# The residual's reordered copies to memory: from GpSimd beside the scans to ScalarE, in part one stage earlier

## The chip, the cores and the metric

The kernel runs on one core of a Trainium2 chip. A core has five instruction streams that run side by side and wait for each other by semaphores: TensorE (PE, with its weight loads as PEld), VectorE (DVE), ScalarE (ACT), GpSimd (POOL) and SyncE (SP), and sixteen DMA engines that serve the transfers issued by SP, ACT and POOL. The metric is the device time of one execution in microseconds.

## The reference, cut to what matters

The program is one step of a two-layer diffusion backbone on 1024 latent tokens and 128 context tokens of width 1024. Layer 0 mixes tokens by a short convolution and a Fourier transform; layer 1 mixes them by a bidirectional state-space scan (S5). Each layer has a gated feed-forward part behind its mixer, and each part adds to the residual `x`:

```python
h = modulate(rmsnorm(x, p['norm1_g'][l]), sh1, sc1)
m, fin = s5_mixer(h, ...)                # layer 1: scans forward and backward
x = x + g1 * m
h = modulate(rmsnorm(x, p['norm2_g'][l]), sh2, sc2)
x = x + g2 * swiglu(h, p['w_ffn_in'][l], p['w_ffn_out'][l])
```

So the residual that leaves layer 0's feed-forward part is read twice: normalised, as the input of the scans, and unchanged, when the scans' gated output is added to it.

## The kernel before, in words

The residual lies in SBUF as `xall`, eight feature tiles (`x[0]` to `x[7]`) of 128 partitions by 1152 tokens. Three chunks of 384 tokens (`CW`, chunk numbers 0 to 2; the last has 256 latent and 128 context tokens) are the unit of work of layer 0.

**End of the feed-forward stage of layer 0.** `last_outer` goes chunk by chunk: for each of eight output tiles TensorE makes six products, VectorE adds them to `xall` (L599, `update`), ScalarE squares the result (L192, tile `sq`, or `ssq` for the first of a chunk), and GpSimd sums the squares (L196). Three `sq` buffers are in use. When a chunk's eight squares are there, TensorE sums them over partitions (L205, `nst`), VectorE makes the reciprocal root in small steps (L207, L163 to L169), TensorE spreads it (L217, `nrb`), VectorE multiplies (L1022, tile `t`, four buffers), and ScalarE scales, shifts and reorders the tokens into `u` (L1025: one instruction of 384 tokens a tile, for the last chunk two of 256 and 128). This last part is `S5In.chunk(ch)`, called through `per_chunk` for chunks 0 and 1, and directly for chunk 2.

**Entry of the scans.** Each complete `u` tile goes to memory (`u_d<-u`, issued by SP) and comes back with another partition layout (`U<-u_d`). The tiles of `u` lie in slots that the scans use later as `D`, `re` and `tp`, so the scans' first writes wait until the stores have read them. `front(f)` makes input products (tile `S`) that ScalarE copies into `D` (L1143, with small start values by L1145 and L1146).

**Scans.** For each of eight feature tiles f, VectorE runs `scan(f)`: six elementwise products and sums (L1151 to L1156), two `TENSOR_TENSOR_SCAN` instructions (L1169), six more of the first kind. The first and last tile go in halves of 584 elements, the others have 1168. `back(f)` makes outputs `Y`, `gelu(f)` writes them over `xall[f]`; so the residual must have left `xall[f]` before. That is what `spill(f)` does: GpSimd copies tile f of the residual in the order of the scans' tokens to a tile `xs` (L1211, 1024 and 128 tokens) and sends it to memory `x_d` (L1213), from where `Glu.load_x` takes it after the scans (L1272). `run` issues `spill(f)` in turn f of its loop, with `issue_after` holding it behind the last sum of squares.

The order on each engine is made by the tile framework, not by the order of the calls alone: it places instructions by when it expects them to be able to run, and adds the waits. ScalarE, VectorE and GpSimd then run their streams strictly in that order.

Of the kernel before, what the change touches and what calls it, by code (L numbers as in the profile page):

```python
# [11 lines left out]
F32 = mybir.dt.float32  # L12
# [7 lines left out]
D = 1024  # L20
# [21 lines left out]
def segments(lo, hi):  # L42
    """the parts of a range of tokens by conditioning."""
    out = []
    if lo < LAT:
        out.append((lo, min(hi, LAT), 0))
    if hi > LAT:
        out.append((max(lo, LAT), hi, 1))
    return out
# [7 lines left out]
def kernel(  # L57
# [30 lines left out]
    # ---------------------------------------------------------------- constants  # L88
# [19 lines left out]
    # ---------------------------------------------------------------- helpers  # L108
# [24 lines left out]
    class Pools:  # L133
# [9 lines left out]
        def s(self, p, dt=F32):  # L143
            """short-lived tiles, apart from the long-lived ones where they have slots of their own."""
            return self.act.tile([128, CW], dt, tag="s", name=nm(p), bufs=self.ns) if self.ns else self.a(p, dt)
# [11 lines left out]
    # rsqrt(v) by Newton from an integer seed  # L157
# [17 lines left out]
    def unpermuted(fn, dst, src, ch):  # L175
        """context tokens back from (t, c) order."""
# [6 lines left out]
    class Norm:  # L183
        """means of squares of a chunk's tokens, three blocks of tokens with one per partition."""
# [28 lines left out]
    def spread(r):  # L213
        """rstd of three blocks of tokens from a column per block to every partition."""
# [5 lines left out]
    def modulated_tile(P, x, rb, f, ch, l, which):  # L220
        """x * rstd * scale + shift of a tile, in its two parts; rb covers the chunk."""
# [10 lines left out]
    def modulated(P, norm, ch, xs, l, which, h):  # L232
        """in parts, a tile each."""
# [8 lines left out]
    # ---------------------------------------------------------------- conditioning  # L242
# [22 lines left out]
    def ada_slice(P, s):  # L265
        """a slice of layer 0's conditioning map, off the tensor engine but for the sum over partitions;
        in two parts, to be issued some time apart. The rows go through memory to one feature per partition."""
# [18 lines left out]
    def ada_columns(l, b0, nb, src, t):  # L286
        """blocks of 128 outputs, from memory to one per partition."""
# [9 lines left out]
    def ada_block(pool, l, s, raw, nrow=2):  # L297
        """in two parts, to be issued some time apart."""
# [11 lines left out]
    def ada_rows(pool, s, raw):  # L310
        """a block of layer 1's conditioning map, the rows of the four groups of products to memory."""
# [8 lines left out]
    def ada_sums(pool, b0, nb):  # L320
        """sums of the four groups, one output per partition."""
# [21 lines left out]
    # ---------------------------------------------------------------- entry  # L343
    def start(P, st, x, h):
        """x to one feature per partition, its norm, modulation and the first two tiles of the
        input projection, a feature tile at a time as the conditioning arrives."""
# [96 lines left out]
    # ---------------------------------------------------------------- layer 0 mixer  # L443
    def mixer(P, big, x, h, norm2, hn, first):
# [10 lines left out]
        def four_in(i):  # L455
# [5 lines left out]
            # folded about 512 and 256: sums of even and odd outputs for cosine, then sine, and the middle  # L461
# [140 lines left out]
    # ---------------------------------------------------------------- feed forward  # L602
    def ffn(P, l, x, h, norm_next, steps=None, nsteps=0, at_end=None, per_chunk=None):
# [32 lines left out]
        def last_outer(j0):  # L636
            """the last two, a chunk of tokens at a time."""
# [25 lines left out]
    # ---------------------------------------------------------------- S5 tables  # L663
# [10 lines left out]
    def exp_poly(pool, x, n):  # L674
        """exp of an fp32 array by range reduction and a polynomial."""
# [21 lines left out]
    def sincos(pool, a, n):  # L697
        """sine and cosine of an fp32 array, reduced by parts of 2 pi that multiply exactly."""
# [36 lines left out]
    def state_layout(dst0, dst1, dup):  # L735
        """[(d, p), g] from dup[(d, g), p twice]."""
# [269 lines left out]
    # ---------------------------------------------------------------- S5 layer  # L1006
    class S5In:
        """modulated input of the S5 layer, a chunk of tokens at a time."""
# [24 lines left out]
    class S5:  # L1033
# [40 lines left out]
        def parts(f):  # L1074
            """the first and the last tile go through in halves."""
# [762 lines left out]
```

## Time and profile before

| what | value |
|---|---|
| time, median of 3 runs | 2558.5 us |
| lowest and highest run | 2555.06 and 2559.73 us |
| profiled execution, first to last instruction (span) | 2550.3 us |
| median less that span | 8.2 us |
| TensorE clock, mean granted | 0.978 of full speed |
| busy: PE, DVE, ACT, POOL | 95%, 70%, 36%, 10% |

The profile is of one execution. The time of that execution itself is not listed apart from the three runs; the 8.2 us between its span and the median lie before the first and after the last instruction, and the sums below are made on the span with these 8.2 us added. A share of busy time is a mean over stages that have different limits, so the stages that the change touches are read by windows and by instructions in order of time.

### The profile page before, as it was taken

How to read it: one execution, taken by the hardware profiler on the slowest of the kernel's cores; microseconds unless marked ns; L12 is line 12 of the kernel's file. 1: busy time of each engine (PE TensorE's matmuls, PEld its weight loads, DVE VectorE, ACT ScalarE, POOL GpSimd, SP SyncE). 2: the span in 40 equal slices, each digit the busy share in tenths (PEclk: the TensorE clock that was granted, in tenths of full speed). 3: DMA queues.
4: the chain of work that ended last, by engine and by line, in shares of the span. 5: the costliest groups of instructions: out<-in, count | busy, mean ns of one | idle time of the engine just before them, and what ended most of it. 6: DMA issues, size and time to landing. Idle time of an engine off the chain costs nothing. (4 is left out here: it accounts for less than half of the span.)

```text
span 2550.3 us, 44262 instructions
## 1 busy us (share of the span) xinstructions
PE 2426.1 (95%) x16815; PEld 2360.4 (93%) x16815; DVE 1789.7 (70%) x4641; ACT 906.2 (36%) x1915; POOL 252.0 (10%) x256
## 2 busy tenths in 40 slices
PE   7999999999999999999956789999999999989998
PEld 6999999999999999999946679998999999989998
DVE  7765678787787778887869984558766666644444
ACT  5322443233222322223364443435232232434333
POOL 0000120000000000000124421112000000122110
PEclk9999999999999999999978889999999999999999
DMA  9443342244444444443457954433222222466543
GB/s 258 127 137 96 92 116 61 68 122 122 123 115 123 122 114 130 115 131 115 116 195 221 261 177 147 120 103 103 74 77 69 88 62 86 147 204 189 162 132 124
DMA packets 503093, 327.96 MB, mean 129 GB/s; under 512 B 99144, under 2 KB 472448, under 8 KB 502880
## 3 DMA queue, kind: packets, MB, share of 16 engines
q1 hardware_dynamic: 330208, 233.10, 30.8%
q10 hardware_dynamic: 163680, 58.96, 9.6%
q0 software_dynamic: 8992, 33.07, 3.9%
q8 instruction: 133, 2.18, 0.4%
q14 instruction: 80, 0.66, 0.1%
HBM read 254.04 MB, written 71.01 MB: 127 GB/s over the span
## 5 line engine op out<-in xcount | busy, mean ns | idle before, releaser
L123 PE MATMUL mm<-hh,whi 128*128 128x384 f32 x1392 | 472.6, 339 | 1.1 <-ACT f L459 1.1
L125 PE MATMUL mm<-hh,wlo 128*128 128x384 f32 x1392 | 466.4, 335 | 0.0
L124 PE MATMUL mm<-hl,whi 128*128 128x384 f32 x1392 | 465.3, 334 | 0.0
L117 DVE TENSOR_TENSOR wlo<-wraw,whi 128x1024 fp32r<-128x1024 f32 (+1 forms) x216 | 259.8, 1203 | 243.5 <-ACT whi L116 240.2
L116 ACT ACTIVATE whi<-wraw 128x1024 fp32r<-128x1024 f32 (+1 forms) x218 | 226.0, 1037 | 506.3 <-PE mm L124 383.5
L123 PEld LDWEIGHTS mm<-hh,whi 128*128 128x128 f32 x1392 | 261.3, 188 | 11.2 <-issue 9.2
L125 PEld LDWEIGHTS mm<-hh,wlo 128*128 128x128 f32 x1392 | 261.3, 188 | 2.9 <-issue 2.5
L124 PEld LDWEIGHTS mm<-hl,whi 128*128 128x128 f32 x1392 | 261.5, 188 | 0.0
L599 DVE SCALAR_TENSOR_TENSOR xall<-mm,modt,xall 128x384 f32<-128x384 f32 (+2 forms) x416 | 203.6, 510 | 60.3 <-PE mm L125 59.4
L123 PE MATMUL mm<-hb,whi 128*128 128x384 f32 x528 | 179.9, 341 | 11.3 <-ACT whi L116 11.2
L1534 PE MATMUL mm<-T,wf 128*128 128x288 f32 x640 | 189.4, 296 | 0.0
L1535 PE MATMUL mm<-T,wf 128*128 128x288 f32 x640 | 188.8, 295 | 0.0
L1536 PE MATMUL mm<-T,wf 128*128 128x288 f32 x640 | 188.2, 294 | 0.0
L125 PE MATMUL mm<-hb,wlo 128*128 128x384 f32 x528 | 179.4, 340 | 2.0 <-DVE wlo L117 1.9
L123 PE MATMUL mm<-hidh,whi 128*128 128x384 f32 x528 | 180.0, 341 | 0.0
L124 PE MATMUL mm<-hb,whi 128*128 128x384 f32 x528 | 178.6, 338 | 0.0
L125 PE MATMUL mm<-hidh,wlo 128*128 128x384 f32 x528 | 176.6, 334 | 0.0
L124 PE MATMUL mm<-hidl,whi 128*128 128x384 f32 x528 | 176.5, 334 | 0.0
L196 POOL TENSOR_TENSOR ssq<-ssq,sq 128x384 f32<-128x384 f32 (+1 forms) x78 | 100.1, 1284 | 686.9 <-ACT sq L192 683.7
L123 PE MATMUL mm<-zz,whi 128*128 128x288 f32 x512 | 151.5, 296 | 2.4 <-ACT zz L1267 2.4
L124 PE MATMUL mm<-zz,whi 128*128 128x288 f32 x512 | 150.8, 295 | 0.3
L125 PE MATMUL mm<-zz,wlo 128*128 128x288 f32 x512 | 150.4, 294 | 0.3 <-DVE wlo L117 0.3
(391 smaller groups left out, 5710.5 us busy)
## 6 DMA issues: line engine op xcount, KB each, us to landing
wraw<-in_w_ffn_out_dram SPq DMA_DIRECT2D x70, 512.0 KB
wraw<-in_w_ffn_in_dram SPq DMA_DIRECT2D x52, 512.0 KB
araw<-in_w_ada_dram ACTq DMA_DIRECT2D x48, 512.0 KB
wraw<-in_w_glu_dram SPq DMA_DIRECT2D x32, 512.0 KB
araw<-in_w_ada_dram ACTq DMA_DIRECT2D x80, 192.0 KB
wraw<-in_w_out_mix_dram SPq DMA_DIRECT2D x24, 512.0 KB
xall<-in_w_ffn_in_dram SPq DMA_DIRECT2D x20, 512.0 KB
wr<-in_w_ffn_in_dram SPq DMA_DIRECT2D x20, 512.0 KB
```

Of the source, the lines that this page charges most:

```text
L116: S.activation(hi[:, :n], raw[:, :n], AF.Copy)
L117: eng.tensor_sub(lo[:, :n], raw[:, :n], hi[:, :n].bitcast(F32))
L123: PE.matmul(ps, wh, xs[0], start=start, stop=False)
L124: PE.matmul(ps, wh, xs[1], start=False, stop=False)
L125: PE.matmul(ps, wl, xs[0], start=False, stop=stop)
L196: self.last = G.tensor_add(self.ssq[ch], self.ssq[ch], sq)
L599: V.scalar_tensor_tensor(x[o][:, a:b], ps[:, a - ch * CW:b - ch * CW], gate(l, which, o, s), x[o][:, a:b], op0=OP.mult, op1=OP.add)
L1534: PE.matmul(ps, wh, xh[:, cs], start=kt == 0, stop=False)
L1535: PE.matmul(ps, wh, xl[:, cs], start=False, stop=False)
L1536: PE.matmul(ps, wl, xh[:, cs], start=False, stop=kt == NFK - 1)
```

## The change

`spill` is made per tile and chunk, on ScalarE. Its copy writes a tile `xs` of 384 tokens from a pool of three buffers of its own; the store is still issued by GpSimd, now as a strided one: for latent tokens, each of eight rows of a tile's image in `x_d` gets 48 tokens (192 bytes) of chunk 0 or 1, or 32 tokens (128 bytes) of chunk 2; the context tokens are one run of 512 bytes. Chunks 0 and 1 are copied in `per_chunk`, in the feed-forward stage right after the chunk's `S5In.chunk`; chunk 2 is copied in the scans' loop. The `yz` pool of the scans has four slots where it had five. The core of the diff (comments taken out of other places are left away):

```diff
-        BUFS = {"U": 3, "T": 4, "d0": 2, "D": 4, "re": 3, "tp": 1, "yz": 5}
+        BUFS = {"U": 3, "T": 4, "d0": 2, "D": 4, "re": 3, "tp": 1, "yz": 4}
...
-        def spill(self, f):
-            xs = self.t("yz", "xs")
-            for a, b in ((0, LAT), (LAT, TOK)):
-                G.tensor_scalar(xs[:, a:b].rearrange("p (t c) -> p t c", t=T8),
-                                self.x[f][:, a:b].rearrange("p (c t) -> p t c", t=T8), 1.0, 0.0, op0=OP.mult, op1=OP.add)
-            nc.gpsimd.dma_start(x_d[f], xs[:, :TOK])
+        def spill(self, f, ch):
+
+            lo, hi = ch * CW, (ch + 1) * CW
+            xs = self.pools[0].tile([128, CW], F32, tag="xs", name=nm("xs"), bufs=3)
+            for a, b, ctx_ in segs(ch):
+                n = (b - a) // T8
+                part = xs[:, a - lo:b - lo].rearrange("p (t c) -> p t c", t=T8)
+                S.activation(part, self.x[f][:, a:b].rearrange("p (c t) -> p t c", t=T8), AF.Copy)
+                base, c0, wd = (LAT, 0, NC_CTX) if ctx_ else (0, a // T8, NC_LAT)
+                dst = x_d[f][:, base:base + T8 * wd].rearrange("p (t c) -> p t c", t=T8)[:, :, c0:c0 + n]
+                nc.gpsimd.dma_start(dst, part)
...
-                with tc.issue_after(self.after):
-                    self.spill(f)
+                self.spill(f, NCH - 1)
...
             def per_chunk(ch):
                 s5["in"].chunk(ch)
+                for f in range(NF):
+                    s5["run"].spill(f, ch)
```

Where the copies come to stand is the framework's doing. On ScalarE, around the end of chunk 1's scaling, the stream of before reads as follows (`u` is the scaled tile, `sq` the square of a residual tile of chunk 2, `d` a decay table that is needed later; the words in brackets are the engines or DMA queues waited for):

```order
L1125 ACTIVATE d_15741<-smask,rho 128x146
L192 ACTIVATE sq_15571<-xall 128x384 [waits DVE_49,Pool_49]
L1125 ACTIVATE d_15741<-smask,rho 128x146
L192 ACTIVATE sq_15611<-xall 128x384 [waits DVE_49,Pool_49]
L1025 ACTIVATE u_15217<-t_15578,modt_87,scalet_89 128x8x48 [waits DVE_49]
...
L1025 ACTIVATE u_15224<-t_15599,modt_87,scalet_89 128x8x48 [waits DVE_49]
L1025 ACTIVATE u_15217<-t_15658,modt_87,scalet_89 128x8x32 [waits DVE_49]
L1025 ACTIVATE u_15217<-t_15658,modt_87,scalet_89 128x8x16
```

And in the changed kernel, at the same place (`L1215` is the new copy; `DMASW` are the stores that GpSimd issues):

```order
L1025 ACTIVATE u_15217<-t_15602,modt_87,scalet_89 128x8x48 [waits DVE_49]
L192 ACTIVATE sq_15595<-xall 128x384 [waits Activation_49,Pool_49]
...
L1025 ACTIVATE u_15224<-t_15623,modt_87,scalet_89 128x8x48 [waits DVE_49]
L1215 ACTIVATE xs_15635<-xall 128x384 [waits DMASW0_49,Activation_49]
L1215 ACTIVATE xs_15638<-xall 128x384 [waits DMASW1_49,Activation_49]
L1215 ACTIVATE xs_15641<-xall 128x384 [waits DMASW2_49,Activation_49]
L192 ACTIVATE sq_15659<-xall 128x384 [waits Pool_49]
L1125 ACTIVATE d_15789<-smask,rho 128x146 x4
L1215 ACTIVATE xs_15644<-xall 128x384 [waits DMASW3_49,Activation_49]
L1215 ACTIVATE xs_15647<-xall 128x384 [waits DMASW4_49,Activation_49]
L1025 ACTIVATE u_15217<-t_15706,modt_87,scalet_89 128x8x32 [waits DVE_49]
```

The last two squares of chunk 2 stood ahead of the eight `u` of chunk 1; now one stands behind the first of them and the last behind all eight and three copies. Ahead of this place the stream has eleven more copies: five between the squares of chunk 1, three behind the eight `u` of chunk 0, three between the squares of chunk 2.

The second place is ScalarE's stream at the entry of the scans. Before, the copies of `S` to `D` for tile 0 followed the start values directly:

```order
L1145 ACTIVATE D_15750<-h_15213 128x2 x3
L1143 ACTIVATE D_15750<-S_15752 128x2x145 [waits PE_49]
...
L1143 ACTIVATE D_15751<-S_15760 128x2x145 [waits PE_49]
L1146 ACTIVATE D_15751<-h_15214 64x2 [waits Activation_49]
L1143 ACTIVATE D_15750<-S_15768 128x2x145 [waits PE_49]
```

Now three pairs of copies of chunk 2 stand ahead of them, and three more pairs between the eight `D<-S` of tile 0, each pair behind the two stores of the pair three before it:

```order
L1145 ACTIVATE D_15798<-h_15213 128x2 x3
L1215 ACTIVATE xs_15972<-xall 128x256 [waits DMASW5_49]
...
L1215 ACTIVATE xs_16293<-xall 128x128
L1143 ACTIVATE D_15798<-S_15800 128x2x145 [waits PE_49]
...
L1143 ACTIVATE D_15799<-S_15808 128x2x145 [waits PE_49]
L1215 ACTIVATE xs_16454<-xall 128x256 [waits DMASW1_49,DMASW0_49]
...
L1143 ACTIVATE D_15798<-S_15848 128x2x145 [waits PE_49]
L1215 ACTIVATE xs_16776<-xall 128x256 [waits DMASW5_49,DMASW4_49]
L1146 ACTIVATE D_15798<-h_15213 64x2 [waits Activation_49]
L1143 ACTIVATE D_15799<-S_15856 128x2x145 [waits PE_49]
```

The last `D<-S` of tile 0, the row at the end, thus stands behind the copy that waits for the third pair's stores. VectorE's and TensorE's streams keep their order, but for a few neighbouring products. On GpSimd the 16 copies and 8 stores of before are replaced by 32 stores (16 of chunks 0 and 1, 16 of chunk 2), all ahead of the first `zp<-yd_d`.

## Rows read from the trace of the kernel before

**Rows 1.** The page, busy time of the engines over the whole span.

```profile
PE 2426.1 (95%) x16815; PEld 2360.4 (93%) x16815; DVE 1789.7 (70%) x4641; ACT 906.2 (36%) x1915; POOL 252.0 (10%) x256
```

**Rows 2.** Windows: length, then busy PE, PEld, DVE, ACT, POOL; PEclk, DMA share, GB/s.

```profile
1270.50:1281.60 11.10, 9.81 (x63) 9.49 (x62) 8.55 (x23) 7.67 (x23) 7.29 (x8) 1.00 0.39 158
1281.60:1297.40 15.80, 9.06 (x55) 8.39 (x53) 13.07 (x35) 13.16 (x22) 6.70 (x7) 0.87 0.50 167
1297.40:1307.60 10.20, 3.13 (x14) 2.68 (x14) 7.56 (x22) 7.89 (x8) 6.25 (x7) 0.50 0.36 109
1317.70:1328.60 10.90, 8.84 (x120) 8.49 (x116) 2.80 (x4) 8.68 (x43) 0.00 (x0) 0.86 1.03 407
1328.60:1506.20 177.60, 127.47 (x992) 121.35 (x992) 177.53 (x137) 66.48 (x234) 70.33 (x27) 0.85 0.78 227
```

**Rows 3.** Timeline of DVE in the scans: start, duration, instruction (us).

```profile
1356.14 1.35 DVE L1156 TENSOR_TENSOR D<-D,D 128x1168 f32<-128x1168 f32 x1
...
1376.53 3.15 DVE L1156 TENSOR_TENSOR D<-D,D 128x1168 f32<-128x1168 f32 x1
...
1466.23 3.15 DVE L1156 TENSOR_TENSOR D<-D,D 128x1168 f32<-128x1168 f32 x1
...
1487.01 2.54 DVE L1155 TENSOR_TENSOR re<-T,re 128x584 f32<-128x584 f32 x1
1489.48 0.98 DVE L1152 TENSOR_TENSOR tp<-T,D 128x584 f32<-128x584 f32 x1
...
1499.70 0.73 DVE L1155 TENSOR_TENSOR re<-T,re 128x584 f32<-128x584 f32 x1
...
1503.64 2.53 DVE L1156 TENSOR_TENSOR D<-D,re 128x584 f32<-128x584 f32 x1
```

**Rows 4.** Timeline of POOL: the copy of residual tile 1.

```profile
1365.62 14.34 POOL L1211 TENSOR_SCALAR xs<-xall 128x1024 f32<-128x1024 f32 x2
```

**Rows 5.** Groups by shape on ACT, 1260 to 1560 us (L939: all): count, busy us, mean ns.

```profile
L1025 ACT ACTIVATE u<-t,modt,scalet 128x384 f32<-128x384 f32 x16 | 16.1, 1087 | 2.4 <-DVE t L1022 2.4
L192 ACT ACTIVATE sq<-xall 128x384 f32<-128x384 f32 x21 | 10.6, 518 | 5.8 <-POOL ssq L196 2.9 <-DVE rq L167 1.8 <-DVE xall L599 0.6
L939 ACT ACTIVATE io<-fx 128x256 f32<-128x256 f32 x64 | 42.0, 708 | 67.3 <-DMA e_d<-io 55.9 <-DMA acol<-ada_d 3.6 <-DVE tt L833 3.5
```

**Rows 6.** Timeline of ACT at the end of the feed-forward stage.

```profile
1274.87 1.02 ACT L1125 ACTIVATE d<-smask,rho 128x146 f32<-128x146 f32 x3
...
1281.63 8.19 ACT L1025 ACTIVATE u<-t,modt,scalet 128x384 f32<-128x384 f32 x8
...
1297.47 7.89 ACT L1025 ACTIVATE u<-t,modt,scalet 128x384 f32<-128x384 f32 x8 [2.39 <-DVE t L1022]
1307.67 10.08 ACT L1025 ACTIVATE u<-t,modt,scalet 128x256 f32<-128x256 f32 x16 [2.31 <-DVE t L1022]
```

**Rows 7.** Timeline of PE and DVE: the sum of squares and the reciprocal root.

```profile
1273.01 0.28 PE L205 MATMUL nst<-ones,ssq 128*128 128x1 f32 x2
...
1274.44 0.16 DVE L207 TENSOR_SCALAR v<-nst 128x3 f32<-128x3 f32 x1 [0.61 <-PE nst L205]
...
1302.00 0.15 DVE L207 TENSOR_SCALAR v<-nst 128x3 f32<-128x3 f32 x1
1302.19 1.00 DVE L163 TENSOR_SCALAR rq<-v 128x3 int32<-128x3 int32 x1
...
1307.08 2.54 DVE L1022 TENSOR_TENSOR t<-xall,nrb 128x384 f32<-128x384 f32 x5 [1.13 <-PE nrb L217]
```

**Rows 8.** Stores and loads issued by POOL (L1272, L1630): ns min/median/max, and landing of L1630.

```profile
L1272 POOL DMA_DIRECT2D xall<-x_d x4: 884/892/917, 1524.8 to 1537.8; - x4
...
L1630 POOL DMA_DIRECT2D hr<-hid_d x46: 537/539/557, 2218.1 to 2431.6; - x46
...
DMA to landing us min/median/max: 2.6/4.3/8.1
```

**Rows 9.** Timeline of DVE at the entry of the scans.

```profile
1328.60 1.44 DVE L1152 TENSOR_TENSOR tp<-T,D 128x584 f32<-128x584 f32 x2 [1.46 <-DMA u_d<-u]
```

## The prediction

> **What bounds the kernel now.** I read the page first: TensorE is busy for 95% of the span, VectorE for 70%, GpSimd for 10% [rows 1]. That is a mean over stages, so I next cut the span into windows around the change [rows 2]. The reader should see three stages. From 1270 to 1297 us TensorE still ends the feed-forward part while ScalarE squares, scales and reorders. From 1297 to 1328.6 us nothing is kept busy: this is a chain of short steps from the last square of chunk 2 to the first scan, and ScalarE's stream is a part of it. From 1328.6 to 1506.2 us VectorE is busy for 177.53 of 177.60 us: the scans are bound by VectorE alone. Behind it, TensorE's next products need the scans' last outputs. So a microsecond added to the chain, or taken from VectorE's scans, is one of the whole; what happens on GpSimd counts only through these two.
>
> **What the change removes: GpSimd's copies beside the scans.** VectorE's own timeline shows their price [rows 3]. The same instruction (`D<-D,D`, 1168 elements) took 1.35 us at 1356.14, where GpSimd had no copy, and 3.15 us at 1376.53 and in each tile up to 1466.23, five times in all. In that time GpSimd's copy is recorded as busy for 14.34 us [rows 4], nearly all of it waiting; it gets through once a tile and then holds VectorE up. The period of a tile without a copy is 1376.53 - 1356.14 = 20.39 us; with one it is (1466.23 - 1376.53) / 4 = 22.43. Five tiles give 5 x 2.04 = 10.2 us. In tile 6 two instructions take 2.54 and 0.98 us, where their kind takes about 0.74 each (0.73 in the row at 1499.70): 2.0 us. In tile 7 one takes 2.53 in place of 0.74: 1.8 us. Together **14.0 us** leave the scans. Nothing else should take the place of VectorE there: ScalarE is busy for 66.48, TensorE for 127.47 of the 177.60 us, the DMA engines for 0.78 of them [rows 2], and the tile from 1356.14 on ran its 20.39 us without a gap.
>
> **What it adds: sixteen copies ahead of the last scaling.** The trace has no such copy, so I bound its price [rows 5]. An instruction of 384 tokens in plain order takes 0.52 us (`sq`), one that reorders as the copy does, but also scales and shifts, 1.09 us (`u`); a plain copy that permutes 256 elements takes 0.71. In a row, instructions start about 0.1 us earlier than the last one ends (eight `u` in 8.19 us, three `d` in 1.02) [rows 6]. The copy has `u`'s strides without its two operands, so I take 0.95 us, a pitch of **0.85 us**, between bounds of 0.43 and 1.01.
>
> Each copy needs one of three buffers, so it also waits for the store of the copy three before it. GpSimd needs 0.89 us to issue a transfer of 1024 pieces [rows 8]. The landing of a transfer of the same size (192 KB) lies between 2.6 and 8.1 us, median 4.3; the pieces of that one are longer, though. I take **4 us after the issue**.
>
> Now the chain on ScalarE, in three stretches.
>
> *To the first `u` of chunk 0 (1281.63).* Five copies, 4.3 us. ScalarE is idle there for 11.10 - 8.55 = 2.6 us [rows 2], and eight small fills of about 2 us in all move further back. The fourth copy waits for the first store and comes about half a microsecond late: **+0.5 us**.
>
> *To the first `u` of chunk 1 (1297.47).* Six copies, 5.1 us, 0.9 us of the fills moved here, 0.9 us for the ninth copy, which waits for the sixth's store, and the 0.5 from before. Against that stands the idle time of 15.80 - 13.16 = 2.6 us: **+4.8 us**.
>
> *To the first `u` of chunk 2 (1307.67).* Before, this took 10.2 us: the eight `u` of chunk 1 and a gap, since the last square of chunk 2 was made earlier and its root waited only for VectorE. In the new order the last square stands behind those eight `u` and three copies, and the chain begins there. So: eight `u` at 1.01, two squares at 0.42, three copies at 0.85 make 11.5 us; then the sum on TensorE 1.4 (1273.01 to 1274.44), the root 2.4, the spread 1.1, the product and its hand-over 0.6 (1307.08 to 1307.67) [rows 6, 7]. The root took 3.95 us before (1307.08 - 1.13 - 1302.00); its first two steps took about 1.0 us each beside GpSimd's fills, 0.8 more than the 0.2 of such a step (1302.00 to 1302.19). The fills now come later, so I count 2.4, with 3.95 as the bound. Sum 17.0 less 10.2: **+6.8 us**. The last two copies, with four fills, take 2.9 us under this chain as long as their stores land in time.
>
> So the last scaling starts 0.5 + 4.3 + 6.8 = **11.6 us** later (the 4.8 contains the 0.5). With it go the stores of `u`, on which the first scan waits [rows 9].
>
> **What it adds at the entry of the scans.** The last `D<-S` of tile 0 stands behind the copy that waits for the third pair of chunk 2's stores. Counted from the end of the last `u`: 1.0 us to the first pair's first half, three pairs of stores at 0.9 + 0.6 us on GpSimd, 4 us of landing, 1.1 us of work, 10.6 us. VectorE needs that tile at its second `tp` product, 0.7 us after 1328.60, 11.5 us after the last `u` ended. At 4 us of landing this costs nothing; but the DMA engines are full just then (share 1.03, [rows 2]), so landings nearer 6 us, and `u`'s own stores delayed by these packets, are likely: 0 to 3 us, I take **+2 us**. The last pairs of copies of chunk 2 and the smaller `yz` pool have VectorE's 20 us per tile to hide in; without that cover the pairs would cost their 2 us. The stores of chunks 0 and 1 need no time of the path beyond the waits counted.
>
> **Sum.** 2550.3 - 14.0 + 11.6 + 2.0 = 2549.9 us of span; with 8.2 us around it, **2558 us**, against a median of 2558.5. The gain in the scans is paid back ahead of them. About 0.2%, or 5 us, is what a measurement of this kernel can tell from no change.
>
> **The rivals.**
>
> *Slow landings (slower).* With three buffers, a copy that waits for its store holds up what stands behind it three times on the path: the fourth copy before a square of chunk 1, the ninth before squares of chunk 2, the fifteenth before the last scaling. Beyond about 4.5 us after the issue, each further microsecond costs three. At 6 us the chain is 16.5 late and the entry 3: 2558.5 + 5.5 = 2564; at 8 us, the upper end of the row, 22.5 and 3: 2570. It decides from 6 us on. For it: stores of 1024 pieces of 192 bytes, when no row of the trace shows one with pieces so short. Against it: at 1281 to 1307 us the DMA engines are half idle (0.50 and 0.36) [rows 2]. The Trainium skill gives a rule for each side in "DMA: Bandwidth & Descriptors": by its fit (section "Anatomy of one DMA — SWDGE (gpsimd) path") such a store would need about 2.0 us plus 0.45, an estimate by which no copy waits and the chain would be 10.7 us late; by its section "Specifications" pieces under 512 bytes are read, modified and written, which would make it longer. The row of 2.6 to 8.1 us [rows 8] bears out neither for such pieces.
>
> *Cheap copies (faster).* If the reordering read costs nothing, a copy has a pitch of 0.43 us. Then the second stretch is +2 us, the third 8.1 + 0.8 + 1.3 + 5.5 - 10.2 = +5.5, and the chain some 7.5 to 8.5 us late. With nothing lost at the entry this is 2558.5 - 14.0 + 8 = 2552.5. The `u` row, twice the plain price, speaks against it.
>
> *The scans don't get shorter.* If loads of the tables or the outputs were the true limit at 22.4 us a tile, the 14 us would not come back, and the time would be 2558.5 + 13.6 = 2572. The tile of 20.39 us and VectorE's lack of any gap speak against it.
>
> **Chances.** No change by the sum above 0.54, slow landings 0.24, cheap copies 0.16, scans not shorter 0.06. In the first case the time lies between 2553.5 and 2563. Slower than by 0.2%: 0.24 + 0.06, less a little for the mild end of slow landings, 0.28; faster 0.17; within it 0.55. The range of 2552.5 to 2567 leaves out the dear end of the slow landings and the last case.
>
> **What would show it.** Right: `D<-D,D` with a mean of 1.36 us in the scans, a tile period of 20.4 us, L1215 at 0.85 to 1.0 us, the first `u` of 256 tokens at about 1319, the second `tp` product at about 1343, the last scan work ending near 1506 as before. Wrong: waits of ScalarE on stores ahead of L1215 of more than a few microseconds in sum; VectorE idle between scans; or the last square of chunk 2 well before 1312.

## The result, and the profile after it

The changed kernel took 2569.5 us in the median of 12 runs (2559.76 to 2578.11); the kernel before, beside it on the same chip, 2556.6 us (12 runs, 2550.61 to 2560.71). The ratio is 1.0054, with a 95% interval of 1.0041 to 1.0066: 14 us slower. The forecast was no change, 2558.0 us; the time lies above the upper end of its range.

The profiled execution of the changed kernel has a span of 2558.9 us and took 2561.05 us, so some 2.2 us lie around a span, not the 8.2 us that the forecast added. By an estimate from that, the profile of before is one of an execution of some 2552.5 us, near the lowest of its runs; sums are better made on differences.

To place the 14 us, the program around the change is cut at seven events that both traces have. Each event is the start of an instruction, but for the last scan work, which is taken at the end of the last `D<-D,re`. The first `tp` product starts at 1328.60 before and at 1349.43 in the changed kernel; the expectation of e11 calls it the second.

| stretch | before | changed | difference | forecast |
|---|---|---|---|---|
| first square of chunk 0 to first `u` of chunk 0 | 17.31 | 19.49 | +2.2 | +0.5 |
| to first `u` of chunk 1 | 15.84 | 20.59 | +4.75 | +4.3 |
| to first `u` of chunk 2 | 10.20 | 17.44 | +7.2 | +6.8 |
| to the first `tp` product | 20.93 | 27.42 | +6.5 | +2 |
| to the end of the last scan work | 177.57 | 168.49 | -9.1 | -14.0 |
| to the first split of the outputs (`zz` on VectorE) | 5.23 | 7.42 | +2.2 | 0 |
| sum | 247.08 | 260.85 | +13.8 | -0.4 |

The sum agrees with the measured difference (13.8 us by the ratio). From `zz` to the end, where both kernels are the same, the changed one's profile happens to be 5.3 us shorter (1033.6 against 1038.9 us); e11 below shows how far that stretch scatters.

VectorE's timeline of the changed kernel in the scans (start, duration, instruction, idle time before it and what ended it); it answers to [rows 3, 9]:

```profile
1347.39 0.77 DVE L1151 TENSOR_TENSOR re<-T,D 128x584 f32<-128x584 f32 x1 [3.58 <-ACT D L1146]
...
1349.43 1.44 DVE L1152 TENSOR_TENSOR tp<-T,D 128x584 f32<-128x584 f32 x2
...
1376.96 1.35 DVE L1156 TENSOR_TENSOR D<-D,D 128x1168 f32<-128x1168 f32 x1
...
1397.35 1.35 DVE L1156 TENSOR_TENSOR D<-D,D 128x1168 f32<-128x1168 f32 x1
...
1478.90 1.35 DVE L1156 TENSOR_TENSOR D<-D,D 128x1168 f32<-128x1168 f32 x1
...
1491.40 0.77 DVE L1151 TENSOR_TENSOR re<-T,D 128x584 f32<-128x584 f32 x1 [4.82 <-ACT y L1188]
...
1517.15 0.77 DVE L1156 TENSOR_TENSOR D<-D,re 128x584 f32<-128x584 f32 x1
1523.05 1.23 DVE L117 TENSOR_TENSOR wlo<-wraw,whi 128x1024 fp32r<-128x1024 f32 x1 [5.14 <-PE Y L1183]
```

The reader is to see that the stall left as forecast: every `D<-D,D` takes 1.35 us, and a tile takes (1478.90 - 1376.96) / 5 = 20.39 us. But VectorE now stands idle for 4.82 us ahead of tile 7, and what follows the scans waits for `Y` for 5.14 us, where it waited 3.33 before:

```profile
1509.49 1.23 DVE L117 TENSOR_TENSOR wlo<-wraw,whi 128x1024 fp32r<-128x1024 f32 x1 [3.33 <-PE Y L1183]
```

ScalarE's timeline ahead of the scans (rows picked from it); it answers to [rows 6]:

```profile
1283.98 8.28 ACT L1025 ACTIVATE u<-t,modt,scalet 128x384 f32<-128x384 f32 x8
1292.11 2.50 ACT L1215 ACTIVATE xs<-xall 128x384 f32<-128x384 f32 x3
...
1299.87 0.89 ACT L1215 ACTIVATE xs<-xall 128x384 f32<-128x384 f32 x1 [2.80 <-DMA x_d<-xs]
...
1304.57 1.07 ACT L1025 ACTIVATE u<-t,modt,scalet 128x384 f32<-128x384 f32 x1
1305.54 0.51 ACT L192 ACTIVATE sq<-xall 128x384 f32<-128x384 f32 x1
1305.95 6.87 ACT L1025 ACTIVATE u<-t,modt,scalet 128x384 f32<-128x384 f32 x7
1312.73 2.43 ACT L1215 ACTIVATE xs<-xall 128x384 f32<-128x384 f32 x3
1315.07 0.51 ACT L192 ACTIVATE sq<-xall 128x384 f32<-128x384 f32 x1
...
1322.01 10.08 ACT L1025 ACTIVATE u<-t,modt,scalet 128x256 f32<-128x256 f32 x16 [2.24 <-DVE t L1022]
...
1332.37 2.74 ACT L1215 ACTIVATE xs<-xall 128x256 f32<-128x256 f32 x6
...
1341.36 0.66 ACT L1215 ACTIVATE xs<-xall 128x256 f32<-128x256 f32 x1 [5.20 <-DMA x_d<-xs]
...
1346.59 0.68 ACT L1215 ACTIVATE xs<-xall 128x256 f32<-128x256 f32 x1 [0.82 <-DMA x_d<-xs]
1347.17 0.19 ACT L1146 ACTIVATE D<-h 64x2 f32<-64x2 f32 x1
1347.26 0.39 ACT L1143 ACTIVATE D<-S 128x290 f32<-128x290 f32 x1
```

From the first of three copies in a row to the square behind them are 2.34 us (1312.73 to 1315.07), a pitch of 0.78 us (0.85 was forecast). The last square of chunk 2 starts at 1315.07, behind eight `u` and three copies, and the last scaling 6.9 us after it. The row of 1341.36 is the expensive one of the entry: three pairs of copies went out without a wait, and the fourth waited 5.20 us for a store. The sixth, at 1346.59, waited 0.82 us more. Behind it stands a start value of tile 0 (L1146, 1347.17), and VectorE's second product, at 1347.39, waits for that. The first `tp` product, which waited for the stores of `u` before [rows 9], starts without a wait. All copies' waits for stores together are in the summary by line (columns as in [rows 8]), the stores' landings in the DMA view of 1272 to 1357 us (count, size, median us from issue to landing):

```profile
L1215 ACT ACTIVATE xs<-xall x32: 412/776/958, 1272.5 to 1353.6; 128x384 f32<-128x384 f32 x16, 128x256 f32<-128x256 f32 x8, 128x128 f32<-128x128 f32 x8
...
  DMA x_d<-xs: 11.6, 7
```

```profile
x_d<-xs POOLq DMA_DIRECT2D x16, 192.0 KB, 3.3
...
x_d<-xs POOLq DMA_DIRECT2D x8, 128.0 KB, 7.1
```

### What idles VectorE ahead of tile 7

The rows below, of the timelines of ScalarE with its queue, GpSimd and TensorE, tell one round of an output tile `y` through memory in the changed kernel:

```profile
1470.21 0.37 ACTq L1190 DMA_DIRECT2D yd_d<-y  x1
...
1484.87 1.06 ACT L1204 ACTIVATE xall<-zp 128x1024 f32<-128x1024 f32 x1 [9.72 <-DMA zp<-yd_d]
...
1486.49 0.53 ACT L1188 ACTIVATE y<-Y 128x435 f32<-128x435 f32 x1
```

```profile
1481.20 0.53 POOL L1198 DMA_DIRECT2D zp<-yd_d  x1 [20.33 <-DMA yd_d<-y]
```

```profile
1487.08 0.85 PE L1183 MATMUL Y<-U,M 128*128 128x145 f32 x2 [5.01 <-ACT y L1188]
...
1490.62 0.69 PE L1187 MATMUL Y<-re,fz 128*128 128x145 f32 x2
```

The store of `y` of tile 4 takes 11.0 us to land, its reload 3.7; `gelu` (L1204) waits for it; behind `gelu` on ScalarE stands the copy of tile 5's `Y`, and TensorE waits for that copy's bank. Behind this wait of 5.01 us TensorE's granted clock is 0.50 (1.2 GHz, from 1486.3 to 1493.1 us), and its products follow each other every 0.24 us, where they came every 0.12 us at 1.00 (from 1476 to 1482); that makes the gap longer, by some 2 us as an estimate from the 4.2 us between 1487.08 and 1491.31. VectorE's first product of tile 7 writes the slot of tile 5's last `re`: it waits, among others, for TensorE, whose last product that reads this `re` ends at 1490.62 + 0.69 = 1491.31, and starts at 1491.40. (The row names ScalarE, which had ended a little earlier.) The stores of `y` for tiles 1 to 5 start at 1400.91, 1424.31, 1448.98, 1470.21 and 1492.76: 21 to 25 us a tile, while the scans take 20.39. Before, the same stores came every 22.7 to 24.3 us beside scans of 22.43. So there are two limits at nearly the same height, and the theory to test is: **the outputs' round takes back a good part of what VectorE gains, and the copies' place on ScalarE does the rest.** The rivals are the forecast's: slow landings throughout, and loads (tables, `U`) as the limit.

### The profile page after: what moved, and what is told of

It is laid out like the page before. It is cut to its first block, busy times and chain, and to the rows that moved or that the text cites. A ratio compares the mean times of both kernels' runs of the same rounds, so it can differ in the third digit from the quotient of the medians.

```text
span 2558.9 us, 44327 instructions
## 1 busy us (share of the span) xinstructions
PE 2423.6 (95%) x16815; PEld 2357.8 (92%) x16815; DVE 1774.6 (69%) x4641; ACT 923.8 (36%) x1947; POOL 206.8 (8%) x264
```

## The experiments

All times are medians beside the kernel before on the same chip (2556.6 us beside the changed kernel, 2557 to 2558 in each set of four); "us" is the ratio less 1, times 2557.

| run | median (runs) | ratio, interval | us |
|---|---|---|---|
| changed kernel | 2569.5 (12) | 1.0054, 1.0041 to 1.0066 | +13.8 |
| e11, the same again | 2574.0 (6) | 1.0069, 1.0054 to 1.0084 | +17.6 |
| e1 eight buffers | 2562.7 (12) | 1.0015, 1.0000 to 1.0030 | +3.8 |
| e2 chunk 2 later | 2568.0 (12) | 1.0032, 1.0018 to 1.0047 | +8.2 |
| e8 contiguous stores | 2565.8 (5) | 1.0042, 1.0027 to 1.0057 | +10.7 |
| e3 `gelu` behind `y` | 2575.1 (6) | 1.0071, 1.0052 to 1.0090 | +18.2 |
| e4 no copies | 2548.7 (9) | 0.9965, 0.9950 to 0.9980 | -8.9 |
| e5 no copies, outputs eased | 2542.0 (5) | 0.9950, 0.9934 to 0.9966 | -12.8 |
| e6 copies on ScalarE in the scans | 2553.7 (12) | 0.9993, 0.9982 to 1.0004 | -1.8 |
| e7 e6, outputs eased, four slots | 2564.2 (9) | 1.0029, 1.0014 to 1.0044 | +7.4 |
| e10 e6, own buffer, one a turn | 2556.8 (12) | 0.9995, 0.9983 to 1.0008 | -1.3 |
| e9 e10, outputs eased | 2543.6 (12) | 0.9955, 0.9941 to 0.9969 | -11.5 |
| e12 before, outputs eased | 2557.6 (12) | 1.0003, 0.9992 to 1.0013 | +0.8 |

And the stretches of the profiled executions, as above (chain: first square of chunk 0 to first `u` of chunk 2; entry: to the first `tp` product; scans; tail: to `zz`):

| run | chain | entry | scans | tail |
|---|---|---|---|---|
| before | 43.35 | 20.93 | 177.57 | 5.23 |
| changed | 57.52 | 27.42 | 168.49 | 7.42 |
| e11 | 57.51 | 27.51 | 168.58 | 9.35 |
| e1 | 50.78 | 23.31 | 176.26 | 11.10 |
| e2 | 57.86 | 21.78 | 177.21 | 9.11 |
| e8 | 51.16 | 24.46 | 170.72 | 12.72 |
| e3 | 56.32 | 27.86 | 163.71 | 16.21 |
| e4 | 41.77 | 21.06 | 171.41 | 8.48 |
| e5 | 42.92 | 21.97 | 163.60 | 8.47 |
| e6 | 41.79 | 20.99 | 175.17 | 10.68 |
| e7 | 42.88 | 21.87 | 185.42 | 8.29 |
| e10 | 41.75 | 21.58 | 176.33 | 7.75 |
| e9 | 43.27 | 20.89 | 163.59 | 7.05 |
| e12 | 43.36 | 21.05 | 177.74 | 9.61 |

**e11: how much one profile can tell.** No edit.

> The changed kernel once more, unchanged, for a second profile and more times: how much of the stages' lengths belongs to one execution. Theory: from the first square of chunk 0 to the last scaling 57 to 58 us again (57.52), from there to the second tp product 26 to 28 (27.42), from there to the first split of the outputs 174 to 184 (175.91), with the spread in that last one, since it holds twenty-odd transfers on which the outputs wait; the median 2566 to 2572. Rival: the first two vary by 5 us as well, and then the parts of the difference can't be told from single profiles.

Chain, entry and scans repeat to 0.1 us, the gap ahead of tile 7 nearly so (4.43 us, and 0.39 a tile earlier). The tail is 1.9 us longer and the rest of the program 9 us (1042.5 us against 1033.6). So for the same program the first three stretches can be read from single profiles; the scatter of the times lies behind them. The median, 2574.0, lies above the expected 2566 to 2572.

That last stretch goes with TensorE's granted clock. From `zz` to the end, first in the changed kernel's profile, then in e11's (columns as in [rows 2]):

```profile
1525.34:2558.90 1033.56, 1006.13 (x7032) 998.70 (x7032) 597.45 (x1142) 372.73 (x691) 114.70 (x135) 0.99 0.40 119
1529.69:2572.20 1042.51, 1011.91 (x7032) 1004.55 (x7032) 597.86 (x1142) 372.86 (x691) 114.82 (x135) 0.98 0.39 118
```

The same 7032 products take TensorE 5.8 us longer at a mean clock of 0.98 than at 0.99, while VectorE, ScalarE and GpSimd are busy for less than half a microsecond longer. In the twelve runs of the changed kernel, too, the three at a mean clock of 0.977 or 0.978 took 2559.8 to 2564.2 us and the three at 0.973 or 0.974 took 2570.3 to 2578.1. So a difference of some microseconds between two medians can be the clock's, and a run of the changed kernel with an edit has two sets to be compared with, +13.8 and +17.6 us.

**e1: more buffers.**

```diff
-            xs = self.pools[0].tile([128, CW], F32, tag="xs", name=nm("xs"), bufs=3)
+            xs = self.pools[0].tile([128, CW], F32, tag="xs", name=nm("xs"), bufs=8)
```

> The changed kernel with eight buffers for the copies in place of three; the stream is planned anew with it: nine copies stand ahead of the scaling of chunk 0, seven ahead of that of chunk 1, all squares of chunk 2 ahead of the scaling of chunk 1. Theory (ScalarE's waits for stores, 2.8 + 0.5 + 0.7 us ahead of the last scaling and 5.2 us at the entry of the scans, are the larger part of what the prediction missed): no wait of L1215 above 0.5 us ahead of the last scaling; its first instruction about 8 us later than before the change in place of 14.3, and the entry costs under 2 us in place of 6.5; the time is 10 to 12 us below that of the changed kernel, before + 2. Rival (the copies' own time of 0.85 us on ScalarE is what counts, the waits only fill gaps): the last scaling still starts 12 to 14 us late, the time stays at before + 10 to 13.

ScalarE at the end of chunk 2's squares:

```profile
1305.88 0.51 ACT L192 ACTIVATE sq<-xall 128x384 f32<-128x384 f32 x1
...
1306.29 7.90 ACT L1025 ACTIVATE u<-t,modt,scalet 128x384 f32<-128x384 f32 x8
1316.31 10.09 ACT L1025 ACTIVATE u<-t,modt,scalet 128x256 f32<-128x256 f32 x16 [0.30 <-DVE t L1022]
```

No copy waits for a store any more; the chain is 7.4 us longer than before instead of 14.2, the entry 2.4 instead of 6.5 (under 2 was expected), and the time falls by 10 us: about the theory's numbers. But its reason holds only for the entry. Ahead of the last scaling, what went is the third stretch, 10.0 us in place of 17.4: the last square stands again ahead of chunk 1's eight `u`, and its root runs under them. The first stretch grew by 3.6 us (nine copies ahead of it), the second fell by 2.9. So the rows point to the copies' number and the order that they bring in, more than to the waits; the edit changes both, and no run parts them. Nor does the profile show the fall of the time: in it scans and tail, 176.26 and 11.10 us, take back all that chain and entry gave, and the four stretches sum to 261.45 us, against 260.85 in the changed kernel. That execution, at 2569.78 us, was the slowest of the twelve.

**e2: chunk 2's copies behind tile 0's `D<-S`.**

```diff
-                self.spill(f, NCH - 1)
+                with tc.issue_after(self.last_d.ins):
+                    self.spill(f, NCH - 1)
```

(`last_d` is the last start value that `front(0)` writes.)

> The changed kernel, with the copies of chunk 2 held behind the last D<-S of tile 0 on ScalarE. Theory (the entry is late because a D<-S of tile 0 stands behind copies that wait for stores): no L1215-type wait ahead of tile 0's last D<-S; VectorE's third product of the scans comes 4 to 6 us earlier than in the changed kernel (1349.43 there, with a last scaling from 1322.01), and the time is 4 to 6 us below it, before + 7 to 9, unless the copies' wait now meets tile 1. Rival (the entry is late because the stores of u share the DMA engines with the copies' stores): the entry stays as late, the time at before + 12 to 14.

The chain is unchanged, the entry falls to 21.78 us, 0.9 above that of before. The edit takes the copies' stores out of the entry as well as the waits; that the waits made it late, not `u`'s own stores, is told by the changed kernel's rows of 1347.39 and 1349.43. By the ratios the time is 5.6 us below the changed kernel's, as expected, with intervals that overlap. In the profiled execution, again the slowest of its twelve (2571.49 us), the scans had gaps of 2.62, 3.41, 1.28 and 5.89 us, which took back more than the entry gave.

**e8: contiguous stores.**

```diff
-                nc.gpsimd.dma_start(dst, part)
+            nc.gpsimd.dma_start(x_d[f][:, lo:hi], xs)
```

> The changed kernel with each chunk's copy sent as one store of 1536 contiguous bytes a partition in place of pieces of 192, 128 and 512 bytes, so that the tokens lie in memory in another order than they are read. Theory (the landing of the short pieces is slow and GpSimd's issue of up to 1.1 us delays its sums): an issue takes 0.5 to 0.6 us, a landing 2.5 to 3.5 us in the median in place of 4.6, ScalarE's waits for stores fall from 11.6 to under 4 us, the time is 5 to 9 us below the changed kernel's, before + 5 to + 9. Rival (the landing is set by the DMA engines' other traffic, not by the pieces): median landing 4 to 5 us, the time within 3 us of the changed kernel's, before + 11 to + 14.

The landings fell, in the DMA view of 1272 to 1350 us:

```profile
x_d<-xs POOLq DMA_DIRECT2D x24, 192.0 KB, 2.2
```

An issue takes 0.54 us, ScalarE's waits fall to 7.5 us (under 4 was expected), chain and entry together by 9.3 us. The time is only 3 us below the changed kernel's, between what the theory and the rival gave and within the scatter, because the scans' gaps (6.9 us) and the tail (12.72) took most of it back. Here too the framework put the last square ahead of chunk 1's `u`, so the 9.3 us are not the landings' alone. The landing fell further than expected; what the pieces cost of the whole time stays open. The Trainium skill ("DMA: Bandwidth & Descriptors", "Anatomy of one DMA — SWDGE (gpsimd) path") gives a fit by which 196608 bytes need 2.0 + 0.45 us, an estimate of 2.45. The contiguous stores nearly agree with it (2.2). In the changed kernel the pieces of 192 bytes took 3.3 us, and those of 128 bytes, while the DMA engines' busy share was 1.02 (1333 to 1347 us), 7.1.

**e4: no copies at all.** Copies and stores of the residual are left out; `load_x` reads `u_d`.

> The changed kernel without any copy or store of the residual (after the scans it loads u in place of the residual's copy, a transfer of the same size, so this leaves a part of the computation out). It shows the most that can be had from the removal. Theory (the scans gain 14 us, of which the round of y through memory takes back 5 to 7): the last scaling starts within 1 us of before, the entry too, D<-D,D takes 1.35 us throughout, and the time is 7 to 9 us below before. Rival (the gap before tile 7 is made by the late entry and the copies there alone): no gap, 13 to 14 us below before.

VectorE's idle times in the scans:

```profile
1428.59 1.38 DVE L1152 TENSOR_TENSOR tp<-T,D 128x1168 f32<-128x1168 f32 x1 [1.71 <-ACT D L1146]
...
1450.80 1.38 DVE L1152 TENSOR_TENSOR tp<-T,D 128x1168 f32<-128x1168 f32 x1 [1.74 <-ACT D L1146]
...
1471.53 0.77 DVE L1151 TENSOR_TENSOR re<-T,D 128x584 f32<-128x584 f32 x1 [4.10 <-ACT y L1188]
```

So taking the copies away brings 9 us, not 14: without any copy the scans shorten by 6.2 us only. It is no upper bound, since the changed kernel's own scans, which start later, shorten by 9.1 us, and e9 below, with all copies made, gains as much or more (11.5 us, with intervals that overlap). From tile 4 on they run at 22 us a tile (1437.53 to 1459.74 for `D<-D,D`), behind `D<-S` that stands behind a `gelu` on ScalarE. ScalarE waits 71.7 us in seven waits for `zp` between 1340 and 1505 us. The gap is not made by the late entry or by the copies: the rival falls.

**e3: the changed kernel, `gelu` behind `y`.**

```diff
-                    z.append(self.gelu(f - 3))
+                    with tc.issue_after(self.last_y.ins):
+                        z.append(self.gelu(f - 3))
```

(`last_y` is the last copy of `Y` to `y` issued so far; the three `gelu` behind the loop are held likewise.)

> The changed kernel, with each gelu held on ScalarE behind the last copy of Y to y of the same turn, so that y's copies no longer wait behind a load of zp. Theory (the idle 4.8 us of VectorE before tile 7 and 1.8 us more behind the scans come from the round of y through memory: store, load, gelu, next y copy, on ScalarE's stream, at 20.3 us a tile as long as a scan tile): VectorE has no gap above 1 us between the scans of tiles 6 and 7 and the time is 5 to 7 us below the changed kernel's, before + 6 to 8. Rival (the gap comes from loads of tables or of U that TensorE waits for): the gap of 4 to 5 us stays, the time too, before + 12 to 14.

The gap is gone, the scans take 163.71 us, all that was forecast. But the time did not fall (+18.2 us, beside +13.8 and +17.6 for the changed kernel):

```profile
1527.21 1.23 DVE L117 TENSOR_TENSOR wlo<-wraw,whi 128x1024 fp32r<-128x1024 f32 x1 [11.54 <-PE Y L1183]
```

VectorE waits 11.54 us for the outputs behind the scans. TensorE's waits between 1440 and 1530 us name the next link, above all `fz`, whose loads may start only when the products of the tile before have read its one buffer (columns: us in total, times, longest):

```profile
PE Y L1187 <- DMA fz<-f_d: 6.6, 3, 2.8
PE S L1139 <- ACT xall L1205: 3.8, 1, 3.8
PE S L1139 <- DMA U<-u_d: 3.5, 1, 3.5
PE Y L1186 <- DMA fz<-f_d: 2.9, 2, 2.7
PE Y L1183 <- DMA M<-m_d: 2.1, 1, 2.1
```

The chain of work that ended last runs through these loads: three of `fz`, of 8.05, 7.31 and 6.94 us, lie on it between 1470 and 1530 us. So the theory was half right: ScalarE's order makes the gap, but taking only that away moves the wait to the end. The rival (loads that TensorE waits for) is a link of the same round.

**e5: no copies, and both links eased.** As e4, with e3's edit and a second set of `fz` tiles, chosen by `f % 2`.

> As the run without copies (a part of the computation is left out: the residual's copy; u is loaded in its place), and in addition each gelu behind y's copies on ScalarE and a second set of the four fz tiles, so that their loads need not wait for the products of the tile before. Theory (behind VectorE's scans a second limit lies at 22 to 24 us a tile: the outputs, by y's round through memory and by the loads of fz; the run without copies got 9 us of 14 or less because of it): with both taken away no gap of VectorE above 1 us, a tile period of 20.4 us throughout, the split of the outputs starts within 6 us of the last scan's end, the time 12 to 15 us below before, 4 to 6 below the run without copies alone. Rival (the loads' bandwidth itself is the limit, the DMA engines being 0.8 to 0.9 busy in the scans): gaps of 1 to 2 us a tile or a late end remain, the time at before - 6 to - 10.

No gap in the scans (163.60 us), and 12.8 us less than before. The split starts 8.5 us behind the scans, not within 6. The loads' bandwidth is not the limit: the same loads pass in 14 us less than before.

**e12: the same easing for the kernel before** (`gelu` behind `y`, two of the four `fz` tiles doubled), copies left on GpSimd.

> The kernel before with its copies left on GpSimd, but with each gelu behind y's copies and half of the fz loads ahead, as in the first run of these four. Theory (with GpSimd's copies VectorE's stalls set the pace of 22.4 us a tile, and the outputs' limit lies at about the same): within 4 us of before on either side, the stalls of 3.15 us still there; so the two limits have to be eased together. Rival (the outputs' limit alone is what binds): 6 to 12 us below before, as without GpSimd's copies.

No change: the row

```profile
1468.05 3.15 DVE L1159 TENSOR_TENSOR D<-D,D 128x1168 f32<-128x1168 f32 x1
```

has its stall, and the scans take 177.74 us. Easing one limit alone, GpSimd's (e4) or the outputs' (e12), gives 9 or 0 us; both give 13.

**e6, e10: the copies on ScalarE, all in the scans.** e6 is the kernel before with

```diff
-                G.tensor_scalar(xs[:, a:b].rearrange("p (t c) -> p t c", t=T8),
+                S.activation(xs[:, a:b].rearrange("p (t c) -> p t c", t=T8),
```

and the copies held behind tile 0's last `D<-S`; e10 gives `xs` a buffer of its own (four `yz` slots) and holds each copy behind the `D<-S` of the tile after.

> The kernel before, with its whole-tile copy on ScalarE in place of GpSimd (two instructions a tile, one store of contiguous rows, five yz slots), tile 0's held behind tile 0's last D<-S: the change without its move to the feed-forward stage. Theory (the chain of ScalarE ahead of the scans is where the change loses; the scans gain only what the outputs' second limit leaves): the first scan starts within 1 us of before, D<-D,D at 1.35 us, and the time is 3 to 9 us below before, that of the run without copies or a little above it. Rival (ScalarE's copies of 1.4 us a tile lengthen the outputs' round, which is at its limit): the time is before + 0 to + 6.

> The run above without its last two parts: only the copies on ScalarE in the scans, one a turn, in a buffer of their own, four yz slots. Theory: the scans stall from tile 4 on behind the outputs' round as in the other run with copies on ScalarE, 0 to 5 us below before. Rival (there the stall came from copies that waited for a slot whose store had not landed; with a buffer of their own it goes): 7 to 12 us below before.

In both, the chain is 1.6 us shorter than before and the entry at most 0.7 us longer, so the early place is what costs there. The scans gain only 1 to 2 us: gaps of 1.58, 1.74, 0.49 and 7.40 us in e6, of 3.56, 1.98 and 6.92 in e10. Both times can't be told from before's. e6 lies between what its theory and its rival gave; e10's rival falls, a buffer of its own does not help by itself.

**e7, e9: the same with the outputs eased.**

> The kernel of the run before this one, with each gelu behind y's copies and a second set of fz tiles (for their room: four yz slots and one tile for the start values). Theory (both limits out of the way, copies in ScalarE's idle time): 9 to 14 us below before, the best of all. Rival (the copies, behind four yz slots that now also carry gelu's later reading, wait and hold D<-S up): before - 3 to + 5.

e7 doubled all four `fz` tiles and paid with a `yz` slot, which `xs` shares there: its copies waited 27.8 us in three waits for stores of `y`, with `D<-S` behind them, and VectorE stood idle for 3.2, 9.3 and 9.1 us. That is the rival's mechanism, and at 7.4 us above before it cost more than the rival gave. e9 is e10 with e3's edit and two of the four `fz` tiles doubled:

```diff
-                    nc.sync.dma_start(self.fz[d][i][64 * d:64 * d + 64], f_d[f, i, 64 * d:64 * d + 64])
+                    nc.sync.dma_start(self.fzs[f % 2][d][i][64 * d:64 * d + 64], f_d[f, i, 64 * d:64 * d + 64])
```

> The kernel before with its whole-tile copies on ScalarE, in the scans, each in one buffer of its own and held behind the D<-S of the tile after; each gelu behind y's copies; and a second tile for two of the four fz tiles, so that half of their loads need not wait for the products of the tile before (one tile for the start values and four yz slots make the room). Theory (the outputs' second limit is what kept the gain of 14 us from showing): no gap of VectorE above 1 us in the scans, D<-D,D at 1.35 us, the time 6 to 13 us below before, more than the 3 us of the copies on ScalarE alone. Rival (the loads' bandwidth or ScalarE's added 1.4 us a tile): gaps as without it, before - 4 to + 4.

```profile
1437.88 1.35 DVE L1160 TENSOR_TENSOR D<-D,D 128x1168 f32<-128x1168 f32 x1
...
1458.27 1.35 DVE L1160 TENSOR_TENSOR D<-D,D 128x1168 f32<-128x1168 f32 x1
...
1495.21 1.22 DVE L117 TENSOR_TENSOR wlo<-wraw,whi 128x1024 fp32r<-128x1024 f32 x1 [2.52 <-DMA yd_d<-y]
```

20.39 us a tile to the end, no gap, and a wait of 2.52 us behind the scans. With 2543.6 us it beats the kernel before by 11.5 us (8 to 15) and the changed one by about 25. The 14 us of the scans are there to be had; they need the copies off GpSimd, off the chain ahead of the scans, and the outputs' round shortened.

## Why the prediction was wrong, step by step

- **"14.0 us leave the scans."** The size of the stall was right: 1.35 us and 20.39 us a tile. "Nothing else should take the place of VectorE there" was the step that failed. It was argued from busy shares and from the one tile that "ran its 20.39 us without a gap", tile 1, when the outputs have not yet run behind. The outputs' round takes 21 to 25 us a tile; it took back 4.9 us in the scans, ahead of tile 7, and 2.2 us behind them. The forecast's third rival, given 0.06, is half of what happened; its test ("VectorE's lack of any gap") could not see a limit hidden behind the one being removed: 22.2 us a tile (e4), against 22.43.
- **Entry, "+2 us".** It was 6.5. The path was right, the count had two terms wrong. It took 4 us from the end of an issue to the landing, and the text itself said that landings nearer 6 us were likely with full DMA engines; the third pair's second store was issued at 1337.09 and landed at 1346.50, 8.9 us after its issue ended. And it let VectorE need what stands behind that copy at its second `tp` product; VectorE needed a start value there at its second product of all (1347.39), 2.7 us ahead of that (1350.11). The two together are 7.6 us; less the 0.9 us of slack that the count had left (10.6 against 11.5), 6.7. In e2, without these copies in the way, all but 0.9 us of the 6.5 goes.
- **First stretch, "+0.5".** It was 2.2. No copy waited for a store there, so the term that was counted measured nothing, and another was left out: the stores stand between GpSimd's sums, and the reciprocal root's small steps on VectorE wait for GpSimd. (The idle time of this stretch was misread as well: 8.55 in [rows 2] is VectorE's; ScalarE's is 7.67, 3.4 us idle in place of 2.6. The sum does not hang on it.) In the changed kernel VectorE's steps and GpSimd's work read

```profile
1276.62 1.43 DVE L167 TENSOR_TENSOR rq<-rq 128x3 f32<-128x3 f32 x1
...
1278.28 1.63 DVE L169 SCALAR_TENSOR_TENSOR rq<-rq,rq 128x3 f32<-128x3 f32 x1
```

```profile
1276.99 1.03 POOL L196 TENSOR_TENSOR ssq<-ssq,sq 128x384 f32<-128x384 f32 x1
1277.95 0.90 POOL L1218 DMA_DIRECT2D x_d<-xs  x1
1278.88 1.00 POOL L196 TENSOR_TENSOR ssq<-ssq,sq 128x384 f32<-128x384 f32 x1
```

  Both steps end with a sum (1278.05 and 1278.02; 1279.91 and 1279.88); a step alone takes 0.14 to 0.16 us. Before, the two slow steps of this root read

```profile
1277.16 0.84 DVE L167 TENSOR_TENSOR rq<-rq 128x3 f32<-128x3 f32 x1
...
1278.24 0.86 DVE L169 SCALAR_TENSOR_TENSOR rq<-rq,rq 128x3 f32<-128x3 f32 x1
```

  A third, L164 at 1275.21, rose from 0.17 to 0.96 us. From the first step of the root to the spread's input this is 1.6 of the 2.2 us (7.26 against 5.64 us). Without copies (e4) it is 5.64 us again; with issues of 0.54 us (e8) still 6.98, so an issue's length is not the cause by itself. The Trainium skill says in "SBUF — State Buffer", "Who interferes with whom", that VectorE and GpSimd share a pair of ports as an exclusive lock; the rows agree. The forecast counted such slow steps for the root of the last scaling and not here.
- **Second and third stretch, "+4.3" and "+6.8".** They were 4.75 and 7.2, right in sum and not in every term. In the second the ninth copy waited 2.80 us, not 0.9. In the third the `u`, squares and copies took 11.0 us, not 11.5, and the sum of squares on TensorE 2.3 (1315.63 to 1317.96), not 1.4: the 1.4 came from rows at a granted clock of 1.00 [rows 2], and here it was 0.50 (1.2 GHz, from 1295.2 to 1336.1 us). The reordered squares and the root (2.3) were sized rightly.
- **"Slow landings"** was not the mechanism ahead of the last scaling, though the time lies near its figure. Landings of chunks 0 and 1 took 3.3 us from the start of the issue in the median, so about 2.4 from its end, where 4 were assumed. Of the three waits that the rival counts one was dear: three stores issued from 1293.35 on took 6.4 to 7.2 us and made the wait of 2.80; the others were none and 0.48 us. At the entry landings were as slow as the rival has them, and cost more than its 3 us.
- **"With 8.2 us around it"** compared a profile of one execution with the median of others. Some 2.2 us lie around a span. In the difference between the two kernels this cancels.

In sum the terms were off by 2.6 (chain), 4.5 (entry), 4.9 (gap) and 2.2 us (tail), 14.2 together, all in one direction. What stays open: what cost e1 and e2 their gain in the scans of the profiled executions, why TensorE's granted clock differs between executions of the same program, and, for e9, how much of its gain is `gelu`'s place and how much the `fz` tiles', which were not tried apart there.

## What to carry to other kernels

Before counting a stall's removal as gain, look for the next limit at the same height: follow the stage's other round (here store, load, `gelu`, copy, products) through one period and compare its length with the new period, not with the old. A tile early in a pipeline that runs without a gap does not show the steady state. And work moved to an idle engine is not free if that engine's stream is a chain: what counts is what stands behind each moved instruction, and whether a wait for memory lies in between.

## What the runs showed of the hardware

- A reordering copy on ScalarE (read with a stride of 32 bytes) takes 0.87 to 0.96 us for 384 tokens, where a square in plain order takes 0.52; for 1024 tokens, in e9, 2.04 to 2.11 us, against 1.06 for a `gelu` of 1024 tokens that reads in plain order.
- GpSimd's issue of a store depends on its pieces: 0.54 us for 128 rows of 1536 bytes, 0.89 us in the median for 1024 pieces of 192 bytes.
- A store of 580 KB of `y` beside the scans' loads took 7.9 to 14.4 us in the changed kernel from its issue to the reload that waited for it (1508.27 to 1516.12 for tile 6, 1424.31 to 1438.73 for tile 2); with the reload it is the larger part of a round of 21 to 25 us.
- Behind a wait of 5.01 us TensorE's granted clock was 0.50 (1.2 GHz) from 1486.3 to 1493.1 us in the changed kernel, and the same products came every 0.24 us in place of 0.12. It was 0.50 from 1295.2 to 1336.1 us too, where TensorE was busy for 10.03 of 40.90 us.
